# Second feed-forward matmul of an encoder trunk as seven block products, in a stage of its own

## Chip, cores and metric

One Trainium2 chip, one core. The metric is the device time of one execution in microseconds (us); lower is better. The kernel computes everything in one launch.

## What is computed

Two encoder layers over two sequences of 512 tokens each, width 1024. Each layer has attention, a recurrent branch, gates, an output projection and a layer norm, and then the part that the change touches:

```python
x = layer_norm(ALPHA * x + mixed @ w_out[l], ln1_g[l], ln1_b[l])
ff = jnp.square(jax.nn.relu(x @ w_ff1[l])) @ w_ff2[l]
x = layer_norm(ALPHA * x + ff, ln2_g[l], ln2_b[l])
```

All is float32. `w_ff1[l]` is 1024 × 4096, `w_ff2[l]` 4096 × 1024.

## The kernel before

Every float32 matmul is made of three: an operand is split into a high part (a cast, ACT, L115) and a low part (the difference, POOL or DVE, L116), and `mm3` (L133) multiplies high by high, high by low and low by high into one PSUM bank. One such instruction has 128 rows of weights and 512 moving columns.

The two sequences are called groups, g = 0 and 1. `Fm` (L140) holds an activation transposed, as high and low tiles in slots of 128 × 2048 called X; `put` (L152) fills it by PE transposes, an ACT cast and a DVE subtract that reads PSUM. `acc` (8 tiles of 128 tokens × 1024) holds the residual. Tiles named raw (three buffers, 128 × 1024) take loads from DRAM; tiles named w (three buffers) hold a split weight.

The feed-forward part of a layer runs as follows. `ff1(f)` (L868) loads 128 columns of `w_ff1` (`load_w`, L121), projects both groups (24 matmuls each), takes relu on ACT (L874), squares on DVE (L875) and splits the result into high (ACT, L876) and low (DVE, L877). `ff2` (L882) multiplies, for a token block j and a half n of the output, the outputs of two or four f with rows of `w_ff2` (`load_w2`, L897) and adds the PSUM bank to `acc` on DVE (L892). The loop (L900 to L918) computes the next two f and then the second matmul of the two before, for 8 j and 2 n, so that both matmuls and the splits of both weights alternate all through the stage. The last four f go together, and `close(j)` (L923), layer norm, store, and in layer 0 `put` for the next layer, follows three blocks behind.

What orders the work: the program is written in the order of the loops, each engine has one queue that runs in order, and a scheduler places instructions on these queues by the buffers' availability. DMAs are issued by the SP queue, with eight semaphores in rotation (DMAHW0 to 7), so a ninth DMA waits for the landing of the first.

## Time and profile before

| what | value |
|---|---|
| runs | 3094.91, 3098.53, 3097.73 us; median 3097.73 |
| profiled execution | 3097.14 us, span 3095.3 us, mean granted clock 0.993 |
| PE, DVE, ACT, POOL busy | 98%, 55%, 32%, 22% of the span |
| moved by DMA | 214.48 MB, mean 69 GB/s |
| feed-forward stage of layer 0, of layer 1 | about 846 to 1550 us, about 2390 to 3087 us |

PE is TensorE, DVE is VectorE, ACT is ScalarE, POOL is GpSimd, SP issues DMAs. The span is the profiled time of the core; what lies between it and the execution's own time is before the first and behind the last instruction. The shares are averages over stages with different limits, so the stage that the change touches has to be looked at by itself. Names like L116 are lines of the kernel before.

### The profile page before, as it was taken

The page shows a single profiled execution, that of the slowest core. Times are in us where ns is not written, and L with a number is a line of the kernel's source. Part 1 is how long each engine was busy: PE and PEld are TensorE (multiplying, and loading weights), DVE is VectorE, ACT ScalarE, POOL GpSimd, SP SyncE. Part 2 cuts the span into 40 slices and gives each one's busy share as a digit, 9 for nine tenths or more (in the row PEclk, how much of TensorE's full clock was granted, in tenths as well). Part 3 has the DMA queues.
Part 4 walks back from the last instruction along what each step waited for, and adds up shares of the span by engine and source line. Part 5 has one row for each costly group of instructions (what it writes and reads, how often), then busy time and mean ns, then how long its engine had stood idle before and what let it go on. Part 6 is the DMA issues. An engine that isn't in the chain of part 4 may idle for free.

```text
span 3095.3 us, 42117 instructions
## 1 busy us (share of the span) xinstructions
PE 3028.3 (98%) x17104; PEld 2466.5 (80%) x17104; DVE 1704.2 (55%) x3025; ACT 990.6 (32%) x1730; POOL 679.7 (22%) x368
## 2 busy tenths in 40 slices
PE   8999999999999999999999999999999999999998
PEld 6777787877888888888877777878878888888887
DVE  5888747026544444444668886570265444444446
ACT  3444547323221221121233444573232212221112
POOL 3222110113122221221142221111231212221211
PEclk9999999999999999999999999999999999999999
DMA  3111222256011111111211112322460111111111
GB/s 125 35 42 42 69 83 66 85 170 221 8 55 55 55 47 42 48 55 41 76 63 35 42 42 69 90 66 97 165 214 1 62 48 55 55 42 41 55 45 65
DMA packets 225121, 214.48 MB, mean 69 GB/s; under 512 B 11936, under 2 KB 180512, under 8 KB 224928
## 3 DMA queue, kind: packets, MB, share of 16 engines
q1 hardware_dynamic: 223056, 207.54, 21.1%
q10 hardware_dynamic: 1872, 4.26, 0.4%
q8 instruction: 134, 2.20, 0.3%
q14 instruction: 59, 0.48, 0.1%
HBM read 171.66 MB, written 33.55 MB: 66 GB/s over the span
## 4 chain that ended last, share of the span: by engine, by line
PE 85%; DVE 9%; DMA 2%; issue 2%; ACT 1%; POOL 1%; SPq 0%; POOLq 0%; DVEq 0%; ACTq 0%
PE mm L136 24%; PE mm L138 23%; PE mm L137 23%; PE mm L841 2%; PE mm L842 2%; PE mm L843 2%; PE sm L672 1%; PE sm L618 1%; PE sm L662 1%; PE sm L332 1%; DVE acc L801 1%; PE sm L458 1%; DVE at L367 1%; DVE st L435 1%; PE sm L455 1%
## 5 line engine op out<-in xcount | busy, mean ns | idle before, releaser
L136 PE MATMUL mm<-X,w 128*128 128x512 f32 x2624 | 1033.8, 394 | 3.7 <-ACT w L115 3.3
L137 PE MATMUL mm<-X,w 128*128 128x512 f32 x2624 | 1028.6, 392 | 0.2 <-DVE X L770 0.2
L138 PE MATMUL mm<-X,w 128*128 128x512 f32 x2624 | 1026.7, 391 | 0.7 <-POOL w L116 0.7
L116 POOL TENSOR_TENSOR w<-raw,w 128x1024 fp32r<-128x1024 f32 (+1 forms) x181 | 406.5, 2246 | 1779.7 <-ACT w L115 1672.2
L136 PEld LDWEIGHTS mm<-X,w 128*128 128x128 f32 x2624 | 493.7, 188 | 111.3 <-issue 3.8
L138 PEld LDWEIGHTS mm<-X,w 128*128 128x128 f32 x2624 | 493.9, 188 | 102.0 <-POOL w L116 1.8
L137 PEld LDWEIGHTS mm<-X,w 128*128 128x128 f32 x2624 | 494.0, 188 | 98.3 <-DVE X L770 0.5
L892 DVE SCALAR_TENSOR_TENSOR acc<-acc,mm 128x512 f32<-128x512 f32 x480 | 324.8, 685 | 229.0 <-PE mm L138 228.6
L136 PE MATMUL mm<-X 128*128 128x512 f32 x960 | 373.5, 389 | 0.0
L138 PE MATMUL mm<-X 128*128 128x512 f32 x960 | 373.5, 389 | 0.0
L137 PE MATMUL mm<-X 128*128 128x512 f32 x960 | 373.5, 389 | 0.0
L875 DVE TENSOR_TENSOR t<-t 128x512 f32<-128x512 f32 x128 | 131.4, 1026 | 419.0 <-ACT t L874 419.0
L874 ACT ACTIVATE t<-mm 128x512 f32<-128x512 f32 x128 | 76.4, 597 | 848.5 <-PE mm L138 848.5
L115 ACT CAST w<-raw 128x1024 fp32r<-128x1024 f32 (+1 forms) x182 | 176.6, 971 | 209.7 <-PE mm L138 98.0
L138 PEld LDWEIGHTS mm<-X 128*128 128x128 f32 x960 | 180.2, 188 | 37.6
L136 PEld LDWEIGHTS mm<-X 128*128 128x128 f32 x960 | 180.2, 188 | 37.5
L137 PEld LDWEIGHTS mm<-X 128*128 128x128 f32 x960 | 180.2, 188 | 37.3
L116 POOL TENSOR_TENSOR X<-raw,X 128x1024 fp32r<-128x1024 f32 x66 | 158.2, 2414 | 190.4 <-ACT X L115 190.4
L877 DVE TENSOR_TENSOR X<-t,X 128x512 fp32r<-128x512 f32 x128 | 148.3, 1159 | 75.4 <-ACT X L876 73.0
L770 DVE TENSOR_TENSOR X<-raw,X 128x512 fp32r<-128x512 f32 x32 | 20.7, 688 | 197.2 <-ACT X L769 197.2
L876 ACT CAST X<-t 128x512 fp32r<-128x512 f32 x128 | 79.4, 620 | 112.2 <-DVE t L875 112.2
L841 PE MATMUL mm<-X 128*128 128x512 f32 x256 | 103.4, 404 | 11.2 <-DVE t L800 11.2
(168 smaller groups left out, 3151.9 us busy)
## 6 DMA issues: line engine op xcount, KB each, us to landing
raw<-in_w_ff_dram SPq DMA_DIRECT2D x128, 512.0 KB
raw<-in_w_in_dram SPq DMA_DIRECT2D x84, 512.0 KB
gates<-gt SPq DMA_DIRECT2D x64, 256.0 KB
t<-gates SPq DMA_DIRECT2D x64, 256.0 KB
raw<-o_sp SPq DMA_DIRECT2D x16, 512.0 KB
raw<-in_w_out_dram SPq DMA_DIRECT2D x16, 512.0 KB
dup<-dup SPq DMA_DIRECT2D x40, 128.0 KB
o_sp<-ox SPq DMA_DIRECT2D x16, 256.0 KB
```

The source lines that it names most:

```text
L115: (first or nc.scalar.copy)(hi, src)
L116: (eng or nc.gpsimd).tensor_tensor(lo, src, hi.bitcast(F32), op=ALU.subtract)
L136: nc.tensor.matmul(ps, ah, bh, start=(i == 0), stop=False)
L137: nc.tensor.matmul(ps, ah, bl, start=False, stop=False)
L138: nc.tensor.matmul(ps, al, bh, start=False, stop=(i == n - 1))
L841: nc.tensor.matmul(pend[j, n], mh, wh, start=(k == 0), stop=False)
L842: nc.tensor.matmul(pend[j, n], ml, wh, start=False, stop=False)
L874: nc.scalar.activation(out=t, in_=ps, func=AF.Relu)
L875: nc.vector.tensor_tensor(t, t, t, op=ALU.mult)
L876: nc.scalar.copy(hd[:, 0, g], t)
L877: nc.vector.tensor_tensor(hd[:, 1, g], t, hd[:, 0, g].bitcast(F32), op=ALU.subtract)
L892: nc.vector.scalar_tensor_tensor(acc[j][:, h], acc[j][:, h], ALPHA if first else 1.0, ps, op0=ALU.mult, op1=ALU.add,)
```

## The change

The hidden dimension is cut into two halves by the parity of the block of 128 rows (i, even or odd f), the tokens by group g, the output columns by half n. With h blocks h0 to h3 (f even g 0, f even g 1, f odd g 0, f odd g 1) and w_ff2 blocks (i, n), Strassen's scheme gets the four output blocks (g, n) from seven block products. A table `PHASES` lists them: the sum of h used, the one or two w_ff2 blocks and the sign between them, and the output blocks into which the product is added.

- The first matmul of all 32 f runs as a stage of its own. `ff1` writes the squares, unsplit, into a page of four blocks. For each pair of f, `combine` makes five sums or differences on DVE, and `spill` writes seven blocks of 128 × 512 to DRAM (`hsp`) with three DMAs.
- `w_ff2` is loaded in 16 blocks of 1 MiB, unsplit, into X slots: eight diagonal ones (`early`, four of them in the last pairs, four behind the loop) and eight off-diagonal ones (`late`).
- Then come 7 products × 16 steps. `operands` loads 128 × 512 of h back from DRAM into the left half of a raw tile. For two blocks, POOL writes their sum into the right half, and ACT and DVE split the whole 1024 columns. For one block, ACT casts both halves, DVE subtracts the left and POOL the right. A step of `products` is 12 matmuls (four token blocks × three), accumulated over the 16 steps in four PSUM banks. Operands are made two steps ahead.
- `fold` adds or subtracts a finished bank to or from `acc` on DVE, for each output block that the product belongs to. Two products (`s+`, `m+`) go on in the banks of the one before.
- The closes of group 1 stand in the last product (after steps 1, 4, 7, 10), those of group 0 behind its last four steps, which run token block by token block. In layer 1 the first projection takes group 1 before group 0, and `Fm` opens its slots when they are first written.

The new functions and loops, with the removed lines of the old loops left out where more than four stood together:

```diff
+PAIRS = DFF // P // 2
+H_M1, H_M2, H_M5, H_M6, H_M7, H_M4, H_M3 = range(7)
+PHASES = (
+    ("m", H_M1, (0, 0), (1, 1), ALU.add, ((0, 0, 1), (1, 1, 1))),
+    ("s", H_M2, (0, 0), None, None, ((1, 0, 1), (1, 1, -1))),
+    ("m", H_M5, (1, 1), None, None, ((0, 0, -1), (0, 1, 1))),
+    ("s", H_M3, (0, 1), (1, 1), ALU.subtract, ((0, 1, 1),)),
+    ("s+", H_M6, (0, 0), (0, 1), ALU.add, ((1, 1, 1),)),
+    ("m", H_M4, (1, 0), (0, 0), ALU.subtract, ((1, 0, 1),)),
+    ("m+", H_M7, (1, 0), (1, 1), ALU.add, ((0, 0, 1),)),
+)
...
+    hsp = [dram.tile([PAIRS, P, 7, 512], F32, name=f"hsp{l}") for l in range(DEPTH)]
...
-                    for g in range(NG):
+                    for g in (range(NG), (1, 0))[l > 0 and p == 0]:
...
+            hid = hsp[l]
+            def page(tile, dt=F32):
+                return tile(dt).rearrange("p (k t) -> p k t", t=512)
+            def ff1(f, out):
                 w = load_w([w_ff1[l][:, f * P:(f + 1) * P]])
-                hd = a_tile().rearrange("p (a g t) -> p a g t", a=2, g=NG)
                 for g in range(NG):
                     ps = project(w, x1, g)
                     t = t512()
                     nc.scalar.activation(out=t, in_=ps, func=AF.Relu)
-                    nc.vector.tensor_tensor(t, t, t, op=ALU.mult)
-                    nc.scalar.copy(hd[:, 0, g], t)
+                    nc.vector.tensor_tensor(out[g], t, t, op=ALU.mult)
+            def combine(h, s):
+                add, sub = ALU.add, ALU.subtract
+                nc.vector.tensor_tensor(s[:, H_M1], h[:, 0], h[:, 3], op=add)
+                nc.vector.tensor_tensor(s[:, H_M2], h[:, 1], h[:, 3], op=add)
+                nc.vector.tensor_tensor(s[:, H_M5], h[:, 0], h[:, 2], op=add)
+                nc.vector.tensor_tensor(s[:, H_M6], h[:, 1], h[:, 0], op=sub)
+                nc.vector.tensor_tensor(h[:, 2], h[:, 2], h[:, 3], op=sub)
+            def spill(p, h, s):
+                nc.sync.dma_start(hid[p][:, H_M1:H_M6 + 1], s)
+                nc.sync.dma_start(hid[p][:, H_M7:H_M4 + 1], h[:, 2:4])
+                nc.sync.dma_start(hid[p][:, H_M3], h[:, 0])
+            w2v = w_ff2[l].rearrange("(k i p) n -> i p k n", i=2, p=P)
+            blocks = {}
+            def load_block(i, n, c, tile):
+                t = page(tile)
+                nc.sync.dma_start(t, w2v[i][:, 4 * c:4 * c + 4, n * 512:(n + 1) * 512])
+                blocks[i, n, c] = t
+            def block(b, k):
+                return blocks[b[0], b[1], k // 4][:, k % 4]
+            early = [(b, c) for c in range(4) for b in ((0, 0), (1, 1))]
+            done = []
+            for p in range(PAIRS):
+                if p >= PAIRS - 4:
+                    for b, c in early[:1]:
+                        load_block(*b, c, a_tile)
+                    early = early[1:]
+                h, s = page(a_tile), page(a_tile)
+                for i in range(2):
+                    ff1(2 * p + i, [h[:, 2 * i + g] for g in range(NG)])
+                combine(h, s)
+                done.append((p, h, s))
+                if len(done) > 1:
+                    spill(*done.pop(0))
+            spill(*done.pop(0))
+            for b, c in early:
+                load_block(*b, c, a_tile)
+            late = [((i, 1 - i), c) for i in range(2) for c in range(4)]
+            def operands(ph, k, tile):
+                _, slot, b0, b1, op, _ = PHASES[ph]
+                raw = raw_tile()
+                nc.sync.dma_start(raw[:, :512], hid[k][:, slot])
+                w = tile()
+                if b1 is None:
+                    src = block(b0, k)
+                    nc.scalar.copy(w[:, 0, :512], raw[:, :512])
+                    nc.scalar.copy(w[:, 0, 512:], src)
                     nc.vector.tensor_tensor(
-                        hd[:, 1, g], t, hd[:, 0, g].bitcast(F32), op=ALU.subtract
+                        w[:, 1, :512], raw[:, :512], w[:, 0, :512].bitcast(F32), op=ALU.subtract
                     )
...
+                    nc.gpsimd.tensor_tensor(w[:, 1, 512:], src, w[:, 0, 512:].bitcast(F32), op=ALU.subtract)
+                else:
+                    nc.gpsimd.tensor_tensor(raw[:, 512:], block(b0, k), block(b1, k), op=op)
+                    split(w[:, 0], w[:, 1], raw, nc.vector)
+                return w
+            def products(ps, w, rows, first, stop):
+                for r in rows:
+                    ts = slice(r * P, (r + 1) * P)
+                    hh, hl = w[:, 0, ts], w[:, 1, ts]
+                    wh, wl = w[:, 0, 512:], w[:, 1, 512:]
+                    kw = dict(skip_group_check=True)
+                    nc.tensor.matmul(ps[r], hh, wh, start=first, stop=False, **kw)
+                    nc.tensor.matmul(ps[r], hh, wl, start=False, stop=False, **kw)
+                    nc.tensor.matmul(ps[r], hl, wh, start=False, stop=stop, **kw)
+            fresh = set()
+            def fold(g, n, r, ps, sign):
+                y = acc[4 * g + r][:, n * 512:(n + 1) * 512]
+                if (g, n, r) in fresh:
+                    if sign > 0:
+                        nc.vector.tensor_tensor(y, y, ps, op=ALU.add)
+                    else:
+                        nc.vector.tensor_tensor(y, y, ps, op=ALU.subtract)
+                else:
+                    nc.vector.scalar_tensor_tensor(y, y, ALPHA, ps, op0=ALU.mult, op1=ALU.add)
+                fresh.add((g, n, r))
+            nxt_x = None if last else Fm(c_tile, lazy=True)
             def close(j):
                 layer_norm(acc[j], gb, fp)
@@ -929,14 +996,58 @@
                         (nc.sync, nc.scalar)[n].dma_start(yout[g][r * P:(r + 1) * P, h], acc[j][:, h])
                 else:
                     nc.sync.dma_start(x_res[j * P:(j + 1) * P, :], acc[j])
...
+                    nxt_x.put(j, acc[j])
+            TAIL = 4
+            END = len(PHASES) - 1
+            steps = [(ph, k) for ph in range(len(PHASES)) for k in range(PAIRS)]
+            ready = []
+            def feed(i):
+                if i < len(steps):
+                    ph, k = steps[i]
+                    tail = ph == END and k >= PAIRS - TAIL
+                    ready.append(operands(ph, k, (lambda: a_tile(F32R).rearrange("p (a n) -> p a n", a=2)) if tail else w_tile))
+            ahead = 2
+            for i in range(ahead):
+                feed(i)
+            later, banks = [], {}
+            for i, (ph, k) in enumerate(steps[:len(steps) - TAIL]):
+                name, _, _, _, _, folds = PHASES[ph]
+                feed(i + ahead)
+                if k == 0 and not name.endswith("+"):
+                    ps = [(mm_ps, sm_ps)["s" in name]() for _ in range(4)]
+                products(ps, ready.pop(0), range(4), k == 0 and not name.endswith("+"), k == PAIRS - 1)
+                if ph == 0 and k >= 4 and late:
+                    b, c = late.pop(0)
+                    load_block(*b, c, c_tile)
+                for _ in range(2):
+                    if later:
+                        later.pop(0)()
+                if k == PAIRS - 1:
+                    todo = [(lambda a=(g, n, r, ps[r], sg): fold(*a)) for g, n, sg in folds for r in range(4)]
+                    if len(folds) == 1:
+                        for t in todo:
+                            t()
+                    else:
+                        later += todo
+                    if ph == 0:
+                        gb = load_ln(ln2_g, ln2_b)
+                if ph == END and k % 3 == 1:
+                    close(4 + k // 3)
+            for i in range(ahead, TAIL):
+                feed(len(steps) - TAIL + i)
+            (g, n, sg), = PHASES[END][5]
+            for r in range(4):
+                for k in range(TAIL):
+                    products(ps, ready[k], (r,), False, k == TAIL - 1)
+                fold(g, n, r, ps[r], sg)
+                if r:
+                    close(r - 1)
+            close(3)
+            if not last:
+                xT = nxt_x
```

Engine order at the place between the stages, on the SP queue. In the names, raw_ is the raw tile of an operand, X_ a slot that takes a block of `w_ff2` or holds a page of h, hsp0 the DRAM tensor of layer 0; L913 to L915 are the spill, L922 the block load, L950 the operand load of `operands`. Before, at the end of the loop, one weight after another:

```order
L127 DMA raw_11559<-in_w_ff1_dram 128x8x128 [waits DMAHW6_49,Pool_49]
L127 DMA raw_11625<-in_w_ff1_dram 128x8x128 [waits DMAHW3_49,Pool_49]
L808 DMA raw_11691<-in_w_ff2_dram 128x1024 [waits DMAHW4_49,Pool_49]
L808 DMA raw_11696<-in_w_ff2_dram 128x1024 [waits DMAHW7_49,Pool_49]
L808 DMA raw_11701<-in_w_ff2_dram 128x1024 [waits DMAHW0_49,Pool_49]
L808 DMA raw_11706<-in_w_ff2_dram 128x1024 [waits DMAHW1_49,DVE_49]
```

Now, at the end of the first matmul of layer 0:

```order
L922 DMA X_9883<-in_w_ff2_dram 128x4x512 [waits DMAHW3_49,PE_49]
L950 DMA raw_9829<-hsp0_70 128x512 [waits DMAHW4_49,DVE_49]
L922 DMA X_9903<-in_w_ff2_dram 128x4x512 [waits DMAHW5_49,PE_49]
L922 DMA X_9923<-in_w_ff2_dram 128x4x512 [waits DMAHW6_49,PE_49]
L922 DMA X_9769<-in_w_ff2_dram 128x4x512 [waits DMAHW7_49]
L913 DMA hsp0_70<-X_9635 128x2048 [waits DMAHW0_49,DVE_49]
L914 DMA hsp0_70<-X_9634 128x1024 [waits DMAHW1_49,DVE_49]
L922 DMA X_9771<-in_w_ff2_dram 128x4x512 [waits DMAHW2_49]
L922 DMA X_9773<-in_w_ff2_dram 128x4x512 [waits DMAHW3_49,DMAHW0_49]
L922 DMA X_9775<-in_w_ff2_dram 128x4x512 [waits DMAHW4_49,DMAHW1_49]
L950 DMA raw_9847<-hsp0_70 128x512 [waits DMAHW5_49,DVE_49]
L950 DMA raw_9865<-hsp0_70 128x512 [waits DMAHW6_49,DVE_49]
```

Loads of `w_ff2` blocks, the last pair's spill and the operand loads now share this queue in this order; with steps counted from 0, raw_9829 is the operand of step 4, raw_9847 that of step 5.

Engine order on DVE at the closes of layer 0. L892 was the addition to `acc`, L175 to L187 (now L198 to L210) are the layer norm, L163 (now L186) is the subtract of `put`. Before:

```order
L892 SCALAR_TENSOR_TENSOR acc_7259<-acc_7259,mm_11883 128x512 [waits PE_49]
L175 BN_STATS s6_12071<-acc_7259 128x6 [waits DVE_49]
L163 TENSOR_TENSOR X_11720<-sm_11913,X_11719 128x4x128 [waits Activation_49]
L163 TENSOR_TENSOR X_11722<-sm_11920,X_11721 128x4x128 [waits Activation_49]
L177 BN_AGGR mv_12074<-s6_12071 128x2 [waits DVE_49]
L185 SCALAR_TENSOR_TENSOR acc_7259<-acc_7259,mv_12074,t512_11711 128x512 [waits DVE_49]
L180 RECIPROCAL rs_12076<-rs_12076 128x1 [waits Activation_49]
L892 SCALAR_TENSOR_TENSOR acc_7342<-acc_7342,mm_11927 128x512 [waits PE_49]
L182 TENSOR_SCALAR nb_12079<-mv_12074,rs_12076 128x1 [waits DVE_49]
L187 SCALAR_TENSOR_TENSOR acc_7259<-acc_7259,rs_12076,t512_11715 128x512
```

Now, in the last product, where L132 is the subtract of a split of 1024 columns:

```order
L210 SCALAR_TENSOR_TENSOR acc_7261<-acc_7261,rs_11670,t512_10103 128x512 [waits DVE_49]
L132 TENSOR_TENSOR w_11701<-raw_11699,w_11701 128x1024 [waits DMAHW5_49,Activation_49]
L209 TENSOR_TENSOR acc_7261<-acc_7261,t512_10101 128x512 [waits Activation_49]
L186 TENSOR_TENSOR X_11682<-sm_11685,X_11681 128x4x128 [waits Activation_49]
L132 TENSOR_TENSOR w_11719<-raw_11717,w_11719 128x1024 [waits DMAHW6_49,Activation_49]
L200 BN_AGGR mv_11756<-s6_11753 128x2
L198 BN_STATS s6_11837<-acc_7427 128x6
L186 TENSOR_TENSOR X_11684<-sm_11692,X_11683 128x4x128 [waits Activation_49]
L203 RECIPROCAL rs_11758<-rs_11758 128x1 [waits Activation_49]
L208 SCALAR_TENSOR_TENSOR acc_7344<-acc_7344,mv_11756,t512_10099 128x512 [waits DVE_49]
L132 TENSOR_TENSOR w_11737<-raw_11735,w_11737 128x1024 [waits DMAHW7_49,Activation_49]
L205 TENSOR_SCALAR nb_11761<-mv_11756,rs_11758 128x1 [waits DVE_49]
```

The additions to `acc` between the layer norms are gone from here, and splits of operands stand between them.

## Rows read from the trace of the kernel before

**Rows 1.** The page: busy time of the engines, and the chain that ended last.
```profile
PE 3028.3 (98%) x17104; PEld 2466.5 (80%) x17104; DVE 1704.2 (55%) x3025; ACT 990.6 (32%) x1730; POOL 679.7 (22%) x368
...
PE 85%; DVE 9%; DMA 2%; issue 2%; ACT 1%; POOL 1%; SPq 0%; POOLq 0%; DVEq 0%; ACTq 0%
```

**Rows 2.** Windows in both feed-forward stages: length, busy (instructions) per engine, PEclk, DMA share, GB/s.
```profile
900.00:1000.00 100.00, 100.00 (x443) 82.77 (x442) 45.69 (x58) 18.39 (x25) 21.48 (x9) 1.00 0.16 48
...
2500.00:2600.00 100.00, 100.00 (x443) 82.81 (x442) 41.62 (x52) 20.60 (x29) 20.32 (x9) 1.00 0.14 43
```

**Rows 3.** Timeline of PE inside ff2: start us, duration us.
```profile
1099.73 0.39 PE L137 MATMUL mm<-X,w 128*128 128x512 f32 x1
...
1102.68 0.39 PE L138 MATMUL mm<-X,w 128*128 128x512 f32 x1
```

**Rows 4.** The page, costliest groups: ACT's cast of a weight tile.
```profile
L115 ACT CAST w<-raw 128x1024 fp32r<-128x1024 f32 (+1 forms) x182 | 176.6, 971 | 209.7 <-PE mm L138 98.0
```

**Rows 5.** Single lines: count, duration ns min/median/max, first and last start us, shapes.
```profile
L116 POOL TENSOR_TENSOR X<-raw,X x66: 2386/2396/2697, 733.8 to 3041.8; 128x1024 fp32r<-128x1024 f32 x66
...
L116 DVE TENSOR_TENSOR X<-raw,X x10: 1209/1215/2041, 727.0 to 3040.8; 128x1024 fp32r<-128x1024 f32 x10
...
L875 DVE TENSOR_TENSOR t<-t x128: 691/693/2245, 856.9 to 3043.9; 128x512 f32<-128x512 f32 x128
...
L877 DVE TENSOR_TENSOR X<-t,X x128: 682/693/2529, 858.3 to 3045.5; 128x512 fp32r<-128x512 f32 x128
...
L186 DVE TENSOR_TENSOR acc<-acc,t x32: 669/684/2272, 783.3 to 3090.3; 128x512 f32<-128x512 f32 x32
...
L188 POOL TENSOR_TENSOR acc<-acc,t x32: 1259/1290/1298, 784.0 to 3091.1; 128x512 f32<-128x512 f32 x32
...
L892 DVE SCALAR_TENSOR_TENSOR acc<-acc,mm x480: 673/686/689, 897.2 to 3086.7; 128x512 f32<-128x512 f32 x160
```

**Rows 6.** Timeline at the end of layer 0: a POOL split and a DVE multiply.
```profile
1549.91 2.39 POOL L116 TENSOR_TENSOR w<-raw,w 128x1024 fp32r<-128x1024 f32 x1 [4.15 <-ACT w L115]
...
1550.57 2.27 DVE L186 TENSOR_TENSOR acc<-acc,t 128x512 f32<-128x512 f32 x1 [0.40 <-ACT acc L184]
```

**Rows 7.** Windows with loaded DMA, columns as above, and the packets around the second.
```profile
5.00:10.00 5.00, 4.50 (x22) 4.00 (x22) 1.64 (x3) 3.43 (x5) 0.00 (x0) 1.00 1.03 402
655.00:665.00 10.00, 10.00 (x45) 8.09 (x44) 5.19 (x8) 5.47 (x11) 0.00 (x0) 1.00 0.88 300
...
DMA packets 2953, 4.67 MB, mean 275 GB/s; under 512 B 238, under 2 KB 1385, under 8 KB 2953
```

**Rows 8.** Windows around a pause of PE, columns as above.
```profile
665.20:668.50 3.30, 0.03 (x2) 0.00 (x1) 3.30 (x6) 0.94 (x2) 0.00 (x0) 1.00 0.59 202
668.60:672.00 3.40, 3.40 (x8) 2.43 (x9) 0.12 (x1) 0.62 (x1) 1.51 (x2) 0.50 0.94 263
```

**Rows 9.** DVE's groups while the closes run, 3049 to 3086.7 us.
```profile
L175 DVE BATCH_NORM_STATS2 s<-acc 128x6 f32<-128x512 f32 x14 | 9.7, 690 | 0.2
...
L185 DVE SCALAR_TENSOR_TENSOR acc<-acc,mv,t 128x512 f32<-128x512 f32 x7 | 5.3, 752 | 0.2
L187 DVE SCALAR_TENSOR_TENSOR acc<-acc,rs,t 128x512 f32<-128x512 f32 x7 | 5.2, 742 | 0.0
L186 DVE TENSOR_TENSOR acc<-acc,t 128x512 f32<-128x512 f32 x7 | 4.8, 684 | 0.0
L182 DVE TENSOR_SCALAR nb<-mv,rs 128x1 f32<-128x1 f32 x7 | 1.5, 213 | 0.2
L177 DVE BATCH_NORM_AGGREGATE mv<-s 128x2 f32<-128x12 f32 x7 | 1.5, 209 | 0.2
L180 DVE RECIPROCAL rs<-rs 128x1 f32<-128x1 f32 x7 | 1.1, 157 | 0.0
```

**Rows 10.** Timeline of the program's end.
```profile
3086.28 0.39 PE L138 MATMUL mm<-X 128*128 128x512 f32 x1
...
3090.35 0.69 DVE L186 TENSOR_TENSOR acc<-acc,t 128x512 f32<-128x512 f32 x1 [0.22 <-ACT acc L184]
```

More of the change, by code (lines that the diff above doesn't have):

```diff
@@ L105, in slots @@
     def slots(pool):
-        return lambda: pool.tile([P, 2048], F32R, tag="X", name="X", bufs=8)
+        return lambda dt=F32R: pool.tile([P, 2048], dt, tag="X", name="X", bufs=8)
     glob.tile([P, 32], F32, name="gap0")
@@ L140, in tile_encoder_trunk, with __init__, open @@
     class Fm:
-        def __init__(self, alloc):
-            self.t = {
-                (g, q, a): alloc().rearrange("p (k t) -> p k t", t=SEQ)
-                for g in range(NG) for q in range(2) for a in range(2)
-            }
+        def __init__(self, alloc, lazy=False):
+            self.alloc, self.t = alloc, {}
+            if not lazy:
+                for g in range(NG):
+                    self.open(g)
+        def open(self, g):
+            for q in range(2):
+                for a in range(2):
+                    self.t[g, q, a] = self.alloc().rearrange("p (k t) -> p k t", t=SEQ)
         def at(self, g, k, a):
@@ L153, in put @@
             g, t0 = divmod(j * P, SEQ)
+            if (g, 0, 0) not in self.t:
+                self.open(g)
             for q in range(2):
@@ L866, in tile_encoder_trunk @@
                 x1.put(j, acc[j])
-            def ff1(f):
+            hid = hsp[l]
+            def page(tile, dt=F32):
+                return tile(dt).rearrange("p (k t) -> p k t", t=512)
+            def ff1(f, out):
                 w = load_w([w_ff1[l][:, f * P:(f + 1) * P]])
-                hd = a_tile().rearrange("p (a g t) -> p a g t", a=2, g=NG)
                 for g in range(NG):
@@ L897, in load_w2 @@
-            def load_w2(f, eng=None, early=False):
-                return load_rows(w_ff2[l][f * P:(f + 1) * P, :], eng, early)
-            NF = DFF // P
-            hid, w2 = {}, {}
-            for f in (0, 1):
-                hid[f] = ff1(f)
-                w2[f] = load_w2(f)
-            for f0 in range(0, NF - 4, 2):
-                nxt = (f0 + 2, f0 + 3)
-                for f in nxt:
-                    hid[f] = ff1(f)
-                if f0 < NF - 6:
-                    for f in nxt:
-                        w2[f] = load_w2(f)
-                for j in range(8):
-                    ff2(j, (f0, f0 + 1), hid, w2, f0 == 0)
@@ L914, in tile_encoder_trunk @@
-            fs = tuple(range(NF - 4, NF))
-            for f in fs[2:]:
-                hid[f] = ff1(f)
-            for f in fs:
-                w2[f] = load_w2(f, (nc.vector, nc.gpsimd)[f % 2], f < fs[2])
-            gb = load_ln(ln2_g, ln2_b)
-            if not last:
-                xT = Fm(c_tile)
+                    nc.gpsimd.tensor_tensor(w[:, 1, 512:], src, w[:, 0, 512:].bitcast(F32), op=ALU.subtract)
+                else:
+                    nc.gpsimd.tensor_tensor(raw[:, 512:], block(b0, k), block(b1, k), op=op)
+                    split(w[:, 0], w[:, 1], raw, nc.vector)
@@ L931, in close @@
                     nc.sync.dma_start(x_res[j * P:(j + 1) * P, :], acc[j])
-                    xT.put(j, acc[j])
-            for j in range(8):
-                ff2(j, fs, hid, w2, False)
-                if j >= 3:
-                    close(j - 3)
-            for j in range(8 - 3, 8):
-                close(j)
+                    nxt_x.put(j, acc[j])
[3 more added lines that the diff above has]
+            ready = []
```

15 lines of the change are left out of this document (removed).

## Prediction

> **What bounds the kernel now.** I read the page's engine totals first: TensorE (PE) is busy 98% of the span, VectorE (DVE) 55%, GpSimd (POOL) 22%; the chain that ended last is 85% PE [rows 1]. Then the windows inside the two feed-forward stages: 443 matmuls in each 100 us, no idle time, clock 1.00, DVE under half busy, 43 to 48 GB/s of DMA [rows 2]. So the stage that the change rebuilds is bound by TensorE's instruction count alone, and a removed matmul is worth the spacing of matmuls there: 13 of them start in 1102.68 − 1099.73 = 2.95 us, 0.227 us each [rows 3].
>
> **What is removed.** Second matmul before: 32 row blocks f × 8 token blocks × 2 halves × 3 = 1536 matmuls per layer. After: 7 products × 16 steps × 12 = 1344. That is 192 fewer per layer, 384 in all: 384 × 0.2267 = **−87.0 us**. A step is now 12 matmuls, 2.72 us.
>
> The row's spacing is that of these very instructions, back to back at the full clock. The Trainium skill (TensorE: Matmul & The Clock Gate, Back-to-back issue gap) gives about 131 ns as the sustained spacing of 512-wide matmuls; by that the removed ones would be worth 384 × 0.131 = 50 us, an estimate from the page, and the forecast would rise by 37 us. The trace disagrees (227 ns), and I keep the row.
>
> **First matmul as a stage of its own: 0.** Per pair of f: 96 matmuls, 21.8 us. Beside it POOL splits two weight tiles (2 × 2.4) [rows 5], ACT casts two [rows 4], DVE has four squares and five sums of 0.69 each (the minima of L875 and L877) [rows 5], 6.2 us, and 2.75 MiB of loads and spills make 132 GB/s against 300 to 402 in loaded stretches [rows 7]. All lie well under 21.8. The hi/lo split of the outputs (one ACT cast and one DVE subtract per block, 4 per pair) leaves this stage.
>
> **Between the stages: +20.** E is the end of the first matmul. The SP queue (first order fence) has, from about E − 5: three late w_ff2 blocks, an early one, the last spill (1.5 MiB), another early one, then two that wait for that spill to land, and behind them the operand load of step 5. That is 7 blocks of 1 MiB and the spill: 8.5 MiB, 8.9 MB. At 402 GB/s [rows 7] it takes 22 us and is done at E + 17; at 300, 30 us and E + 25. Then the add, cast and split of step 5: 1.29 (a POOL add, L188) and 1.21 (a DVE split, L116) [rows 5] and a cast of 1.0 [rows 4], 3.5 us. PE gets there at 5 × 2.72 = E + 13.6. So it stalls 7 us at the fast rate, 15 at the slow one. I take 10 per layer, nearer to the fast rate since all these transfers have rows of 2 KB and more, while half the packets around the slow rate were smaller [rows 7]; ends 5 (the blocks get a head start) and 20. After a pause of 3.3 us the trace shows the clock at 0.50 (1.2 GHz) for some 3.4 us [rows 8], which is in the upper end. Both layers have the same order: 2 × 10.
>
> **A two-block step: 0.** Five of seven products need the sum of two weight blocks, 5 × 16 × 2 = 160 steps in which POOL adds 512 columns and DVE subtracts 1024. They exclude each other: a DVE multiply of two SBUF tiles (L186), 0.68 us alone, took 2.27 us beside a POOL split and ended 0.54 us after it [rows 6]; the subtract L877 reaches 2.53 for a median of 0.69, and POOL's split 2.70 for 2.40 [rows 5]. DVE work that reads PSUM never stretches (L892: 673 to 689 over 480) [rows 5]. So the pair costs 1.29 + 1.21 = 2.50 us of a step's 2.72. It fits with 0.22 us to spare, and the three raw and three w buffers hold the chain load, add, cast, split of two steps ahead. I take 0; the upper end is 0.32 us per step (below, +51). The single-block steps (512-wide splits on POOL and DVE, ACT two casts) ask for less.
>
> **Folds: +2.** Two products (M6 and M7) go on in banks just folded; PE waits for the last DVE fold, 0.69 us [rows 5] (its line L892) behind a split at worst: 0.5 each, 2 per layer, 2 layers.
>
> **The last product with the closes: +22.** A layer norm costs DVE 2 × 0.69 + 0.75 + 0.74 + 0.68 + 0.21 + 0.21 + 0.16 = 4.13 us [rows 9], POOL 1.29. Four of them now stand between splits (second fence), one per three steps, 8.16 us of PE. What excludes each other there: POOL 3 adds and the norm's add, 4 × 1.29 = 5.2; DVE 3 splits and the three two-tile operations 0.75 + 0.74 + 0.68, 5.8; together 11.0, 2.8 too much, 11 us over four closes. If the two scalar-tensor ones (1.49 of it) do not exclude POOL, 9.5 and 5 us; if every hand-over waits for ACT too, 15. Middle: 10 per layer, and 1 of half clock after each run of pauses. Before, DVE had the same closes with nothing on POOL but their own adds, and PE lost nothing there.
>
> **Behind the last product.** Layer 0: DVE still has a fold, two closes and three pairs of transposed copies (0.68 each, as L186) [rows 5], some 13 us, while PE has 24 matmuls of the other sequence and four groups of transposes, 9 us: **+4**. Program end: the last matmul ends at 3086.7, DVE's last operation at 3091.0, 4.4 later [rows 10]. Now fold, two closes and their waits for ACT follow the last matmul: 0.69 + 8.3 + 1.5 = 10.5: **+6**.
>
> **Sum.** −87 + 20 + 2 + 22 + 4 + 6 = −33. Against the profiled execution's 3097.1 us that is 3064.1; the median of the runs shown is 0.6 above it: **3065 us**. With the ends of the terms (transition 10 to 40, last product 10 to 32, the rest −3 to +6) all at once, 3040 to 3101 are reached; taken one at a time, about 3050 to 3080, the forecast's own range.
>
> **Rivals.**
> (a) The waits are mostly covered (buffers two steps ahead, loads that start at E − 8): half of the 54 us stays, **3038**. For it: DMA idles at 16% before E [rows 2]; against: the queue order is fixed. 0.15.
> (b) The transition runs at the slow rate with the clock at half behind it, 20 per layer: **3085**. For it: 300 GB/s is what 10 us of mixed loads gave [rows 7]. 0.17.
> (c) DVE and POOL become the bound in the two-block products, and the kernel is slower. If each hand-over costs the 0.54 us that DVE ended after POOL [rows 6] on top of the pair's 2.50, a step is 3.04 us, 0.32 over PE's 2.72, × 160 = +51: **3116**. It decides from 33 / 160 = 0.21 us per step on, a step of 2.93. For it: only 0.22 us to spare, and in-order queues in which DVE's split waits for ACT; against: in the rows the 0.54 lies inside DVE's own 0.68, so it is no addition. 0.15.
> (d) The remaining matmuls lie further apart, so that each removed one is worth 50 us / 384 = 0.131 instead of 0.227: **3102**. The sustained figure of the page named above would give this; against it stands that the same instructions fill every window at 0.226 [rows 2]. 0.02.
> (e) The closes cost twice what I put, 44: **3087**, or with (b) 3107. 0.06.
> The forecast has 0.45.
>
> **How the numbers follow.** A measurement of this kernel can tell about 0.2%, 6 us, from no change, that is 3091.5 to 3103.9. Faster: forecast, (a), (b), half of (e) and a little of (c), 0.82. Same: parts of (c), (d), (e), 0.05. Slower: most of (c), rest, 0.13. The range 3032 to 3100 leaves out (c) and the tails.
>
> **What would show it.** Step by step: 2,688 product matmuls in place of 3,072, spaced 0.227 in the product stages; PE idle of 5 to 20 us some 14 us behind the last first-matmul, released through POOL or ACT from the operand's load; none in the two-block products (a mean step of 2.72 us over products 4 to 6); pauses of 1 to 3 us between splits and layer norms in the seventh; DVE's last operation some 10 us behind the last matmul. The prediction is wrong if a two-block step takes over 2.9 us, if PE in the seventh product loses over 20 us, or if the transition shows no pause.

## The result, and the profile after

The changed kernel takes 3065.84 us (median of 4 runs, 3064.09 to 3066.84) against 3098.13 us (4 runs, 3094.91 to 3099.11): a ratio of 0.9897, interval 0.988 to 0.9914, 32 us or 1.0% faster. The prediction said 3065. The profiled execution took 3064.09 us with a span of 3062.3, 33.0 below the span before.

The page of the changed kernel, as [rows 1]:

```profile
PE 2956.7 (97%) x16720; PEld 2399.4 (78%) x16720; DVE 1666.7 (54%) x2877; ACT 1090.9 (36%) x1826; POOL 865.8 (28%) x532
...
PE 81%; DVE 10%; DMA 3%; issue 3%; POOL 1%; ACT 1%; SPq 0%; ACTq 0%; POOLq 0%; DVEq 0%
```

PE has 384 instructions fewer and is idle 105.6 us (span less busy) where it was idle 67.0. POOL and ACT work more, the chain is still PE's.

Windows of the changed kernel, as [rows 2] (length, busy per engine and instructions, PEclk, DMA share, GB/s): the first matmul alone, the first five steps of the products, the stretch with step 5, products 1 to 6, the last product, and in layer 1 products 1 to 6, the last product, the program's end.

```profile
853.00:1202.20 349.20, 349.20 (x1550) 289.27 (x1549) 134.28 (x152) 70.90 (x101) 86.16 (x35) 1.00 0.40 142
1202.20:1215.70 13.50, 13.50 (x61) 11.08 (x60) 6.08 (x7) 3.65 (x4) 5.73 (x3) 1.00 1.04 405
1215.70:1228.00 12.30, 6.40 (x21) 4.51 (x20) 4.74 (x4) 3.99 (x4) 4.85 (x3) 0.72 0.82 291
1228.00:1471.00 243.00, 243.00 (x1074) 201.05 (x1073) 116.90 (x124) 96.62 (x121) 117.53 (x90) 1.00 0.40 119
1471.00:1539.00 68.00, 54.26 (x235) 42.99 (x234) 56.21 (x78) 27.55 (x39) 34.97 (x20) 0.92 0.38 119
...
2752.00:2995.00 243.00, 243.00 (x1073) 200.90 (x1072) 115.06 (x126) 97.26 (x122) 117.56 (x90) 1.00 0.39 116
2995.00:3048.40 53.40, 46.70 (x187) 35.10 (x185) 47.26 (x64) 18.13 (x24) 27.33 (x16) 0.97 0.32 103
3048.40:3062.30 13.90, 0.00 (x0) 0.00 (x0) 9.34 (x19) 2.84 (x5) 3.80 (x3) 0.61 0.34 132
```

The first matmul and products 1 to 6 have no idle time at all, at clock 1.00, and 1074 matmuls in 243 us are the 0.226 us of before. Almost all losses lie in three places: at step 5 of the first product, in the last product, and behind the last matmul of a layer. PE's pauses in the first two, from PE's timelines of both layers (start, duration, form, and in brackets the idle time before and who ended it):

```profile
1215.61 0.39 PE L973 MATMUL mm<-w 128*128 128x512 f32 x1
1221.86 1.22 PE L971 MATMUL mm<-w 128*128 128x512 f32 x2 [5.86 <-ACT w L131]
...
1484.67 1.12 PE L180 MATMUL sm<-ident,acc 128*128 128x128 f32 x4 [2.58 <-POOL acc L211]
...
1495.55 0.66 PE L180 MATMUL sm<-ident,acc 128*128 128x128 f32 x4 [2.21 <-POOL acc L211]
...
1516.98 1.11 PE L180 MATMUL sm<-ident,acc 128*128 128x128 f32 x4 [4.24 <-POOL acc L211]
...
3021.82 0.50 PE L972 MATMUL mm<-w 128*128 128x512 f32 x1 [1.52 <-DVE w L132]
...
3035.56 0.50 PE L971 MATMUL mm<-X 128*128 128x512 f32 x1 [1.86 <-ACT X L131]
```

The time of a product, from its first matmul to the next one's, in us (an ideal one has 192 × 0.2267 = 43.5):

| layer | 1 | 2 | 3 | 4 | 5 | 6 | last |
|---|---|---|---|---|---|---|---|
| 0 | 51.5 | 43.5 | 43.5 | 43.5 | 43.6 | 43.5 | 67.6 |
| 1 | 51.3 | 43.5 | 43.5 | 43.5 | 43.6 | 43.5 | 54.7 |

The last product of layer 0 also holds 40 transposes of the next layer's input; in the kernel before, 32 stood beside its last second-matmul blocks.

From the last matmul of the output projection to the last one of the second feed-forward matmul (start to start), layer 0 went from 704.8 to 689.8 us (−15.0), layer 1 from 701.2 to 676.6 (−24.5); the stretch between them changed by −2.2, the end by +5.3 (9.0 to 14.3 us behind the start of the last matmul), and what precedes the first stage, whose code is as before, by +3.5. Together −32.9.

### The profile page after: what moved, and what is told of

Same layout as the page of the kernel before. It is cut to its first block, busy times and chain, and to the rows that moved or that the text cites. A ratio compares the mean times of both kernels' runs of the same rounds, so it can differ in the third digit from the quotient of the medians.

```text
span 3062.3 us, 42748 instructions
## 1 busy us (share of the span) xinstructions
PE 2956.7 (97%) x16720; PEld 2399.4 (78%) x16720; DVE 1666.7 (54%) x2877; ACT 1090.9 (36%) x1826; POOL 865.8 (28%) x532
## 4 chain that ended last, share of the span: by engine, by line
PE 81%; DVE 10%; DMA 3%; issue 3%; POOL 1%; ACT 1%; SPq 0%; ACTq 0%; POOLq 0%; DVEq 0%
PE mm L152 17%; PE mm L154 16%; PE mm L153 16%; PE sm L971 3%; PE sm L972 3%; PE sm L973 3%; PE mm L972 3%; PE mm L971 3%; PE mm L973 3%; PE mm L864 2%; PE mm L866 2%; PE mm L865 2%; PE sm L695 1%; PE sm L641 1%; PE sm L685 1%
## 5 line engine op out<-in xcount | busy, mean ns | idle before, releaser
L132 POOL TENSOR_TENSOR w<-raw,w 128x1024 fp32r<-128x1024 f32 (+1 forms) x179 | 417.9, 2336 | 1370.9 <-ACT w L131 1255.2
L131 ACT CAST w<-raw 128x1024 fp32r<-128x1024 f32 (+1 forms) x330 | 332.1, 1007 | 365.4 <-PE sm L973 106.7
L902 DVE TENSOR_TENSOR X<-t 128x512 f32<-128x512 f32 x128 | 88.6, 692 | 427.8 <-ACT t L901 427.8
L961 POOL TENSOR_TENSOR raw<-X 128x512 f32<-128x512 f32 x160 | 221.8, 1388 | 263.6 <-DVE w L132 259.4
L132 DVE TENSOR_TENSOR w<-raw,w 128x1024 fp32r<-128x1024 f32 x153 | 195.7, 1283 | 168.9 <-ACT w L131 168.7
L971 PE MATMUL mm<-w 128*128 128x512 f32 x480 | 190.2, 397 | 11.3 <-ACT w L131 11.3
L972 PE MATMUL mm<-w 128*128 128x512 f32 x480 | 190.3, 396 | 3.7 <-DVE w L132 3.6
L973 PE MATMUL mm<-w 128*128 128x512 f32 x480 | 189.1, 394 | 0.0
L971 PE MATMUL sm<-w 128*128 128x512 f32 x384 | 149.5, 389 | 0.0
L973 PE MATMUL sm<-w 128*128 128x512 f32 x384 | 149.4, 389 | 0.0
L972 PE MATMUL sm<-w 128*128 128x512 f32 x384 | 149.4, 389 | 0.0
L971 PEld LDWEIGHTS mm<-w 128*128 128x128 f32 x480 | 91.7, 191 | 32.0 <-ACT w L131 12.6
L864 PE MATMUL mm<-X 128*128 128x512 f32 x256 | 103.9, 406 | 11.2 <-DVE t L823 11.2
L959 POOL TENSOR_TENSOR w<-X,w 128x512 fp32r<-128x512 f32 x64 | 85.4, 1334 | 98.8 <-ACT w L955 98.6
```

The lines of the kernel that those rows point to most:

```text
L131: (first or nc.scalar.copy)(hi, src)
L132: (eng or nc.gpsimd).tensor_tensor(lo, src, hi.bitcast(F32), op=ALU.subtract)
L864: nc.tensor.matmul(pend[j, n], mh, wh, start=(k == 0), stop=False)
L902: nc.vector.tensor_tensor(out[g], t, t, op=ALU.mult)
L959: nc.gpsimd.tensor_tensor(w[:, 1, 512:], src, w[:, 0, 512:].bitcast(F32), op=ALU.subtract)
L961: nc.gpsimd.tensor_tensor(raw[:, 512:], block(b0, k), block(b1, k), op=op)
```

## The experiments

Each is the changed kernel with the edit shown. The line numbers of PE's matmuls and of the loads move by a few lines with an edit. Times of single runs (tie_late, tie_all, pool256, dveadd, m5last, spread7p) stand beside 3065.8. The kernels that ran four or five times scatter by 1.4 to 7 us, so a few us between single runs tell nothing by themselves; the readings rest on the stretches of the traces.

### tie_late: the off-diagonal blocks later

A one-column copy from a later operand into the block's slot keeps the scheduler from hoisting the load.

```diff
-            def load_block(i, n, c, tile):
+            def load_block(i, n, c, tile, after=None):
                 t = page(tile)
+                if after is not None:
+                    nc.vector.tensor_copy(t[:, 0, :1], after[:, 0, :1].bitcast(F32))
...
-                if ph == 0 and k >= 4 and late:
+                if ph == 1 and k % 2 == 0 and late:
                     b, c = late.pop(0)
-                    load_block(*b, c, c_tile)
+                    load_block(*b, c, c_tile, ready[-1])
```

> The eight off-diagonal w_ff2 blocks are loaded during the second product instead of around the end E of the first matmul; nothing else. In the changed kernel PE stands still 5.9 and 5.4 us from E + 13.6 on. Theory Q (step 5's operand load waits for the bytes queued ahead of it): three 1 MiB blocks fewer stand ahead; from the last spill (about E + 3) on still 4.5 MiB are ahead, 11.7 us at 405 GB/s, so the operand comes at about E + 14.5 and step 5 at E + 18: the pause shrinks to about 4 us per layer, the run to 3060 to 3064 us. Rival S (the pause is the chain spill, landing, slot, block load, whatever else is queued): pauses stay 5.4 to 6, time 3065 to 3067.

Measured: 3066.71 us, pauses of 6.2 and 4.8 us. The rival's numbers. The SP queue's issues, first of the changed kernel, then of tie_late (L913 and L914 the last spill, L922 or L924 the diagonal blocks, L950 or L952 the operand loads):

```profile
1205.12 0.34 SPq L913 DMA_DIRECT2D hsp<-X  x1
1205.72 0.34 SPq L914 DMA_DIRECT2D hsp<-X  x1
1206.11 5.86 SPq L922 DMA_DIRECT2D X<-in_w_ff_dram  x3
1212.40 1.68 SPq L950 DMA_DIRECT2D raw<-hsp  x3
```

```profile
1204.73 0.33 SPq L913 DMA_DIRECT2D hsp<-X  x1
1205.34 0.33 SPq L914 DMA_DIRECT2D hsp<-X  x1
1205.70 5.53 SPq L924 DMA_DIRECT2D X<-in_w_ff_dram  x3
1211.35 1.65 SPq L952 DMA_DIRECT2D raw<-hsp  x3
```

In both the spill is issued at about 1205, 3 us behind the first matmul's end, the last diagonal block 6 us later (its slot holds the page that is being spilled), and the operand load only then. ACT's cast of step 5 starts at the same time in both, ended by that load. From ACT's timelines, the changed kernel first:

```profile
1220.77 2.94 ACT L131 CAST w<-raw 128x1024 fp32r<-128x1024 f32 x3 [11.79 <-DMA raw<-hsp]
```

```profile
1220.68 2.94 ACT L131 CAST w<-raw 128x1024 fp32r<-128x1024 f32 x3 [12.09 <-DMA raw<-hsp]
```

The three off-diagonal blocks went out before the spill, when the DMA engines had room: windows of tie_late show 186 GB/s from 1200 to 1205 us, where the changed kernel has 408. They cost nothing that shows. Theory Q's count, from the spill on at 405 GB/s, was short all the same. Windows behind the spill (DMA share and GB/s last), three of the changed kernel and the first one of tie_late:

```profile
1205.00:1210.00 5.00, 5.00 (x24) 4.14 (x23) 3.95 (x5) 2.11 (x2) 3.09 (x2) 1.00 1.04 423
1210.00:1215.00 5.00, 5.00 (x24) 4.14 (x23) 0.23 (x1) 0.00 (x0) 2.63 (x2) 1.00 1.03 385
1215.00:1220.00 5.00, 1.00 (x5) 0.50 (x3) 0.00 (x0) 0.00 (x0) 0.00 (x0) 0.85 1.05 406
```

```profile
1205.00:1210.00 5.00, 5.00 (x23) 4.13 (x22) 3.80 (x4) 1.93 (x2) 3.48 (x2) 1.00 0.90 307
```

In the changed kernel the DMA engines are full from the spill until the operand is there. In tie_late they have less to do, but the first 5 us run at 307 GB/s, while two block loads wait for the slots of the page being spilled, as the rival has it.

### tie_all: the last two diagonal blocks later too

```diff
-            for b, c in early:
+            for b, c in early[:2]:
                 load_block(*b, c, a_tile)
+            early = early[2:]
...
+                if ph == 0 and k >= 5 and early:
+                    b, c = early.pop(0)
+                    load_block(*b, c, a_tile, ready[-1])
```

> As tie_late, and the last two diagonal blocks (needed from step 12 on) are loaded after the operands of steps 6 and 7, so that only one 1 MiB block and the last spill stand ahead of step 5's operand. Theory Q: from E + 3 on 2.5 MiB, 6.5 us at 405 GB/s, operand at about E + 10, no pause at step 5 in either layer and no half clock behind it: 2 x (5.7 + 3.4) = 18 us less than the changed kernel, about 3048 us. A rival by which step 5 waits for its own chain (spill to DRAM and back, raw buffer, add, cast, split) leaves a pause of 3 us or more and a time over 3055.

Measured: 3046.97 us, 19 less. The first product takes 45.3 and 44.0 us instead of 51.5 and 51.3, and no half clock follows. SP's issues and what is left of PE's pause:

```profile
1203.08 0.33 SPq L913 DMA_DIRECT2D hsp<-X  x1
1203.68 0.33 SPq L914 DMA_DIRECT2D hsp<-X  x1
1204.05 1.22 SPq L924 DMA_DIRECT2D X<-in_w_ff_dram  x1
1205.37 3.17 SPq L953 DMA_DIRECT2D raw<-hsp  x3
```

```profile
1215.08 1.19 PE L974 MATMUL mm<-w 128*128 128x512 f32 x4 [1.12 <-ACT w L131]
```

The operand loads are issued at 1205.37 and step 5 starts on time but for 1.1 us. So the two blocks that stand between the spill and the operand load in SP's queue were the pause. The edit takes away two things at once, their 2 MiB of transfer and the operand load's wait behind them in the queue, so it does not divide the pause between theory Q (bytes) and rival S (the wait for the slots); the windows above fit both.

### pool256: more of POOL's work in a two-block step

```diff
                     nc.gpsimd.tensor_tensor(raw[:, 512:], block(b0, k), block(b1, k), op=op)
+                    nc.gpsimd.tensor_tensor(raw[:, 512:768], block(b0, k)[:, :256], block(b1, k)[:, :256], op=op)
```

> POOL does half of each two-block sum a second time (256 more columns, same values), about 0.7 us more per two-block step: 2.0 us of POOL in a step of 2.72. Theory of exclusion (POOL's two-input add and DVE's 1024-column subtract cannot run at once): 2.0 + 1.21 = 3.2 us per step, 0.5 over PE's 2.72, on about 150 steps: +75 us, some 3140. Rival (they only have to follow each other within the buffers, and POOL has room up to 2.72): no change beyond 10 us, 3066 to 3076.

Measured: 3107.81 us, +42: between the two, and above what "no exclusion" allows. The two-block products in columns 4 to 6 of the table take 44.8, 46.0 and 48.0 us in both layers. Once the buffers' lead is used up a step settles at 2.94 us: in product 6 of layer 0, 15 of the 16 take 2.89 to 2.98 us. The rest are waits for the folds on DVE at the start of products 5 and 7 (0.8 and 1.9 us each), which the changed kernel does not have. POOL's two lines (minimum, median, maximum), and one step of DVE and POOL in product 6:

```profile
L961 POOL TENSOR_TENSOR raw<-X x160: 1269/1293/2290, 1153.8 to 3072.7; 128x512 f32<-128x512 f32 x160
...
L962 POOL TENSOR_TENSOR raw<-X x160: 722/1603/1705, 1155.1 to 3075.0; 128x256 f32<-128x256 f32 x160
```

```profile
1458.84 1.29 POOL L961 TENSOR_TENSOR raw<-X 128x512 f32<-128x512 f32 x1
1459.99 1.23 DVE L132 TENSOR_TENSOR w<-raw,w 128x1024 fp32r<-128x1024 f32 x1 [1.71 <-ACT w L131]
1460.21 1.60 POOL L962 TENSOR_TENSOR raw<-X 128x256 f32<-128x256 f32 x1
```

The added half costs 0.72 alone and 1.60 in the median, with DVE's subtract (1.23) beside it: 0.88 of blocking. One step is 1.29 + 1.60 and small gaps, POOL without a pause. From these rows I estimate the changed kernel's pair at 1.29 + 0.88 and gaps of 0.1, about 2.25 us, not my 2.50: part of DVE's subtract runs beside POOL after all. Of the +42, products 4 to 6 hold some 16 us over both layers, the last product 20 (76.8 and 65.2), the first 3.

### dveadd: the layer norm's last add on DVE

```diff
-    def layer_norm(y, gb, st):
+    def layer_norm(y, gb, st, eng=None):
...
-        nc.gpsimd.tensor_tensor(b, b, gb[1][1], op=ALU.add)
+        (eng or nc.gpsimd).tensor_tensor(b, b, gb[1][1], op=ALU.add)
...
-                layer_norm(acc[j], gb, fp)
+                layer_norm(acc[j], gb, fp, nc.vector)
```

> The last operation of the second layer norm (the add of the bias to the upper half) goes from POOL to DVE, 0.69 us there. Theory T (in layer 0 PE stands still because the transposes of the next layer's input wait for that add, which is queued on POOL behind the operands' sums): PE's pauses in the last product of layer 0 fall from 13 us to under 7, 8 to 12 us less with the clock, about 3056 us; layer 1, without transposes, changes by 2 us at most. Rival X (DVE and POOL together have too much to do, whoever does the add): the pauses of layer 0 stay at 11 us or more, those of layer 1 grow, time 3064 to 3072.

Measured: 3055.27 us. What PE waited for in the last product of layer 0 (total us, times, longest), in the changed kernel and in dveadd:

```profile
PE sm L180 <- POOL acc L211: 11.9, 5, 4.2
PE sm L180 <- DVE mv L200: 1.6, 1, 1.6
```

```profile
PE sm L180 <- DVE mv L200: 2.7, 1, 2.7
PE sm L180 <- DVE acc L210: 2.6, 4, 1.1
PE sm L180 <- DVE acc L211: 0.6, 2, 0.3
```

Theory T's numbers hold in layer 0: the last product goes from 67.6 to 57.3 us. The add was late for two reasons there, and the edit removes both. POOL in the changed kernel, ahead of the transposes of 1484.67:

```profile
1480.74 1.67 POOL L961 TENSOR_TENSOR raw<-X 128x512 f32<-128x512 f32 x1 [2.55 <-DVE w L132]
1482.38 2.24 POOL L211 TENSOR_TENSOR acc<-acc,t 128x512 f32<-128x512 f32 x1
```

The add stands behind an operand's sum, and it takes 2.24 us where its median is 1.29, beside a DVE subtract of a split. In layer 1 it fell from 54.7 to 49.6 as well, where T allowed 2 us and X expected a rise: the edit takes two things away there, the add's time on POOL, which excludes DVE's, and its place in POOL's queue ahead of the next operand's sum, and which of them counted this run does not tell. Of these 15 us some 5 came back behind the layer: from the last product matmul of layer 0 to the first of layer 1 it is 1191.4 us instead of 1185.8. Of these 5.6 us, 2.2 are there within 25 us of the layer's end, where the transposes now wait for DVE:

```profile
1538.78 0.63 PE L180 MATMUL sm<-ident,acc 128*128 128x128 f32 x4 [1.70 <-DVE acc L211]
1542.78 1.09 PE L180 MATMUL sm<-ident,acc 128*128 128x128 f32 x4 [3.38 <-DVE acc L210]
```

Of the rest, 3 us come at two stretches of half clock (3.4 us each, near 1668 and 1750 us) that the changed kernel does not have; why they occur stays open.

### m5last, best_dve, best_put: closes beside other products

m5last changes the order of the products, so that the single-block one comes last, and with it the PSUM banks and the last folds:

```diff
 PHASES = (
-    ("m", H_M1, (0, 0), (1, 1), ALU.add, ((0, 0, 1), (1, 1, 1))),
-    ("s", H_M2, (0, 0), None, None, ((1, 0, 1), (1, 1, -1))),
-    ("m", H_M5, (1, 1), None, None, ((0, 0, -1), (0, 1, 1))),
+    ("s", H_M1, (0, 0), (1, 1), ALU.add, ((0, 0, 1), (1, 1, 1))),
+    ("m", H_M2, (0, 0), None, None, ((1, 0, 1), (1, 1, -1))),
...
     ("m+", H_M7, (1, 0), (1, 1), ALU.add, ((0, 0, 1),)),
+    ("s", H_M5, (1, 1), None, None, ((0, 0, -1), (0, 1, 1))),
 )
...
-                fold(g, n, r, ps[r], sg)
+                for g, n, sg in PHASES[END][5]:
+                    fold(g, n, r, ps[r], sg)
```

> The order of the products alone is changed: M5, whose operand needs one weight block (POOL subtracts 512 columns, DVE subtracts 512), comes last, so the four closes of group 1 stand, at the same steps, beside single-block steps; DVE then has 0.6 us less per step, POOL has as many instructions as before. In the changed kernel the last product takes 67.6 us (layer 0) and 54.7 us (layer 1) against 43.5 for the others. Theory X (POOL and DVE together have too much to do beside the closes): about 60 and 48 us, time some 3052 us. Theory T (the wait is the order in POOL's queue: the norm's add waits there for DVE and holds the next operand's POOL work behind it, and the transposes wait for the add): 64 or more and 53 or more, time 3062 to 3068.

Measured: 3067.57 us. The time is T's, the products are not: the last takes 55.3 and 43.5 us, but M7 before it 48.4 and 49.9, because the scheduler moves layer norms forward to where their data are ready, and group 1 is complete one product earlier (the first of its layer norms now runs 5 us into M7). Together 103.7 and 93.4 us against 111.1 and 98.2. What was won went at the end of layer 0 (1198.6 us to the first product matmul of layer 1 instead of 1185.8), most likely because each token block now needs two folds before its close. The stretch at the boundary, changed kernel first, then m5last:

```profile
1538.80:1560.00 21.20, 17.94 (x76) 13.94 (x75) 13.82 (x26) 8.23 (x14) 9.52 (x12) 0.84 0.33 125
```

```profile
1532.90:1553.40 20.50, 11.06 (x35) 8.12 (x36) 14.68 (x27) 5.97 (x11) 6.69 (x8) 0.50 0.21 82
...
1533.49 1.09 PE L180 MATMUL mm<-ident,acc 128*128 128x128 f32 x4 [2.73 <-DVE acc L210]
...
1540.72 1.09 PE L180 MATMUL mm<-ident,acc 128*128 128x128 f32 x4 [3.66 <-DVE acc L210]
...
1545.38 1.09 PE L180 MATMUL mm<-ident,acc 128*128 128x128 f32 x4 [1.10 <-DVE acc L210]
```

Pauses of 1.1 to 3.7 us between groups of transposes, and the granted clock at 0.50 (1.2 GHz) for 20.5 us, where the changed kernel has 0.84 in the mean. Neither theory had this.

best_dve has this order, the edits of tie_late, tie_all and dveadd, and two closes beside M7, two beside M5:

```diff
-                if ph == END and k % 3 == 1:
-                    close(4 + k // 3)
+                if (ph, k) in {(5, 4): 4, (5, 11): 5, (6, 2): 6, (6, 7): 7}:
+                    close({(5, 4): 4, (5, 11): 5, (6, 2): 6, (6, 7): 7}[ph, k], (None, mm_ps)[ph == END])
```

> tie_dve, and the closes spread: the order of the products is M1, M2, M3, M6, M4, M7, M5, so group 1 is complete after M4, and its four closes stand in the last two products (two beside M7, two beside M5), seven steps apart instead of three. In dveadd the last two products took 43.5 + 57.3 (layer 0) and 43.5 + 49.6 us (layer 1). If the closes only need room: about 43.5 + 48 and 43.5 + 45, some 13 us less than tie_dve, 3020 to 3027 us. Rival (a close costs PE its pause wherever it stands beside two-block steps, or transposes wait in PE's queue anyway): 3033 or more.

best_put moves the transposes of these closes five or six steps back, the edit being a second table of steps for `put`:

```diff
+            CLOSES = {(5, 4): 4, (5, 11): 5, (6, 1): 6, (6, 5): 7}
+            PUTS = {(5, 10): 4, (6, 1): 5, (6, 6): 6, (6, 10): 7}
```

> best_dve, with the transposes of the four closes of group 1 in layer 0 placed five or six steps behind their layer norm instead of right behind it. If transposes that stand in PE's queue before their layer norm is done are what is left of layer 0's pauses: 3 to 6 us less than best_dve. If nothing is left there: the same within 2 us.

Measured: 3048.60 us (3045.39 to 3050.29) and 3047.01 (3046.37 to 3047.78): far above the 3020 to 3027 expected of best_dve, no better than tie_dve below, and alike within 2 us. The last two products take 100.9 and 90.8 us in best_dve; at the boundary of layer 0 it lost 13 us as m5last did. The place of the transposes was not what was left.

### tie_dve and spread7: the repairs together, and another order

tie_dve has the edits of tie_late, tie_all and dveadd, and no other.

> Both repairs together: the block loads held back as in tie_all, and the norm's last add on DVE as in dveadd. Alone they gave 19 and 10.5 us against the changed kernel's 3065.8. If the pauses between the stages and those beside the closes are independent: 3034 to 3040 us. If one repair only moves waiting to the other place: over 3044.

Measured: 3042.66 us (3038.4 to 3045.4, 4 runs), ratio to before 0.9812 (0.9796 to 0.9829). It lies above the 3034 to 3040 of independent gains and below 3044: most adds up. The boundary's 7 us (1192.7 against 1185.8) are not what is missing, since dveadd alone has 1191.4. In the profiled executions some 4 us lie ahead of the first product, where the code is the same (it starts at 1204.2 here, at 1200.2 in tie_all, 1201.9 in dveadd, 1202.2 in the changed kernel), and 4 in the last products, 57.2 and 51.2 us where the single gains would give 54.9 and 49.4.

spread7 takes the two lessons: closes beside a single-block product, and a last product with one fold per block.

```diff
+    ("s", H_M1, (0, 0), (1, 1), ALU.add, ((0, 0, 1), (1, 1, 1))),
+    ("m", H_M2, (0, 0), None, None, ((1, 0, 1), (1, 1, -1))),
+    ("s", H_M3, (0, 1), (1, 1), ALU.subtract, ((0, 1, 1),)),
+    ("s+", H_M6, (0, 0), (0, 1), ALU.add, ((1, 1, 1),)),
+    ("m", H_M4, (1, 0), (0, 0), ALU.subtract, ((1, 0, 1), (0, 0, 1))),
+    ("s", H_M5, (1, 1), None, None, ((0, 0, -1), (0, 1, 1))),
+    ("m", H_M7, (1, 0), (1, 1), ALU.add, ((0, 0, 1),)),
...
+            CLOSES = {(5, 4): 4, (5, 7): 5, (5, 10): 6, (5, 13): 7}
```

> tie_dve with another order: M1, M2, M3, M6, M4, M5, M7. M4 is folded into both of its blocks and M7 no longer goes on in its banks, so group 1 is complete after M4, its four closes stand beside the single-block product M5 (three steps apart), and the last product is M7 with one fold per token block and no close before its last four steps. In best_dve and m5last the last product (there the single-block one) took 43.5 us in layer 1, so the closes then need no pause of their own; what they lost was in M7 beside them (47.3) and, in layer 0, at the end, where M5 has two folds per block (52.7 to 55.3). If those two are what was left: M5 about 48 (layer 0, transposes included) and 44, M7 about 50 and 45, against 43.5 + 57.2 and 43.5 + 51.2 in tie_dve: 10 to 14 us less than its 3042.7, 3028 to 3034 us. If the closes need their pauses anyway or the layer boundary takes them: 3040 or more.

Measured: 3035.02 us (3032.73 to 3038.39, 5 runs), one above the expected range; ratio to before 0.979, interval 0.9776 to 0.9803: 2.1% faster than before, 31 us below the changed kernel. M5 with the closes takes 49.3 and 46.3 us, M7 49.4 and 43.5, and the boundary 1191.7, as with one fold per block in dveadd. What PE still waited for over M5 and M7 of layer 0:

```profile
PE sm L180 <- DVE acc L211: 2.3, 1, 2.3
PE sm L180 <- DVE acc L210: 2.0, 1, 2.0
PE mm L180 <- DVE acc L211: 0.8, 1, 0.8
```

> spread7 with the norm's last add left on POOL. If with the closes beside single-block steps the place of that add no longer matters: within 3 us of spread7. If transposes still wait for it in POOL's queue, as beside the two-block product: 6 to 10 us more, with PE's pauses in layer 0 before transposes.

The edit is spread7 without that of dveadd. Measured: 3044.27 us. The last two products take 103.4 and 91.9 us against 98.7 and 89.8, so 7 of the 9 us lie there: the place of the add still counts (one run), and the longest pause, 5.8 us, again stands before transposes.

## Why the prediction was right

The total was 3065 against 3065.84, with terms that partly cancel.

- **The removed matmuls, −87.0.** As predicted: 384 fewer, and products 2 to 6 take 43.5 us each. The spacing is the row's 0.227 in both kernels, and rival (d) falls. The 131 ns of the Trainium skill (TensorE: Matmul & The Clock Gate, Back-to-back issue gap) are not seen here either.
- **The first matmul alone, 0.** 349.2 us without idle time.
- **Between the stages, +20: measured 15.8** (51.5 and 51.3 against 43.5). Pause and place are as said: 13.6 us behind the start, 5.9 and 5.4 us, ended by the operand load, with some 2 us more lost to the half clock. The transfers ran at 385 to 423 GB/s, near the 402 of the fast rate, and the pause is near the 7 us that it gave, not my 10; the slow rate of rival (b) does not occur. One step of the working was wrong without being felt: I counted 8.9 MB from E − 5 on, with three off-diagonal blocks. tie_late shows that these cost nothing. What counts is the queue from the spill on, issued at E + 3, with the blocks that wait for its slots. My count gives a cast at E + 18.3, and it came at E + 18.4 (1220.77, E being 1202.4); the count of tie_late, from the spill on, gives E + 15.8. Rival (a) leaned on the DMA engines' 16% in the kernel before; in the changed one it is 40% in the first matmul and full behind it.
- **Two-block steps, 0.** Right, 243 us without a pause. The margin was larger than I said: about 2.25 us of 2.72 by the estimate from pool256, so rival (c) was further off than its 0.22 us.
- **Folds, +2: measured 0.** No pause stands at products 4 to 5 or 6 to 7; a step there takes 0.1 us longer.
- **The last product, +22: measured about 32.** What the stages lost beyond the 43.5 saved in each is 28.5 and 19.0 us; less 8.0 and 7.8 at step 5 it is 20.5 in layer 0 and 11 in layer 1. (The table's 24.1 for layer 0 is 3.6 more: the 32 transposes that stood in this stage before as well.) Layer 1's 11 is my term, waits for DVE's splits between layer norms. In layer 0 the wait was another one: transposes of the next layer's input, in PE's queue, held by the norm's add on POOL (11.9 of 13.7 us of pauses). I had counted POOL's time but not that PE itself would stand in line behind it; dveadd shows it. With 20 us lost there my own sign of being wrong (over 20 us in the seventh product) was just reached in layer 0: there the term had the wrong path, and rival (e)'s 44 was about as far off as my 22.
- **Layer boundary, +4: measured −2.2.** There were 3.3 us of pauses (the longest 2.1) and 6.8 us of half clock as I feared (3.4 us lost); but the kernel before had a pause of 1.6 us there too, its two stretches of half clock in layer 1's first part (6.8 and 3.4 us, near 1607 and 1686 us) did not occur, and eight transposes had moved ahead of the boundary. **Program end, +6: measured 5.3.**

So the forecast was right in what carried it, the value of a matmul and the three places of loss, and the sum was right to a microsecond by chance: the last product's 10 us too little and 3.5 of scatter in a part that did not change stood against 4 too much in the transition, 2 in the folds, 6 at the boundary and 1 at the end.

## What to carry to other kernels

When arithmetic is removed from a bound engine, price it by the spacing of its instructions in that stage, then walk through the seams: the queue order at the change of stage and whatever now shares an in-order queue with the next operands. A wait on one queue is paid by everything behind it, so look for instructions that wait for a slow chain (a spill's slot, a layer norm) ahead of loads or sums that the bound engine needs next; here two such places held 30 us, as much as the whole gain. Repair them one by one and look at the next seam each time: part of the second gain came back at the layer boundary.
